# Where the first two block loads are issued, and in which order eight additions stand: a decoder layer on one core

## The chip, the cores and the metric

One core of a Trainium2 chip runs the whole program. The metric is the device time in microseconds. All products run on TensorE (PE); VectorE (DVE), ScalarE (ACT) and GpSimd (POOL) prepare and finish them; SyncE (SP) issues nearly all loads. Each engine works through its own instructions in order, and waits for others by semaphores.

## The reference

One layer of a post-norm decoder on 256 tokens of width 2048, in float32:

```python
def reference(x, w_in, ...):
    ...
    mixed = token_mixers(x, l, w_in[l], ...)   # sparse attention, mLSTM, differential attention
    x = layer_norm(ALPHA * x + jnp.einsum('bse,ed->bsd', mixed, w_out[l]), ln1_g[l], ln1_b[l])
    h = jnp.square(jax.nn.relu(jnp.einsum('bsd,df->bsf', x, w_up[l])))
    x = layer_norm(ALPHA * x + jnp.einsum('bsf,fd->bsd', h, w_down[l]), ln2_g[l], ln2_b[l])
```

The sparse attention scores all keys with a small indexer (8 heads) and keeps the 64 best of each query. The feed-forward part is 8192 wide.

## The kernel before

**Split products.** Each 1 MB piece of a weight is loaded by SP into a buffer `raw` (`load_raw`, L100; three buffers). `split_to` (L107) makes two float32r halves of it: ACT casts `hi` (L108), DVE subtracts `lo = raw - hi` (L109). Both have four buffers. PE multiplies `hi` and `lo` with the split activations. A unit of transposed output (`unit_t`, L203, products L211 and L212) or of normal output (`run_units`, L247, L261 to L263) takes a weight in two halves, and after each half `tick()` moves small work on: whatever a head has put off with `later`, and one step of `block_sums`:

```python
def tick():                     # L87
    ...
    if clock[0] > START:        # L93
        next(blocks, None)
```

**The index.** Early on, while the values of the sparse attention are projected (weights `w_va0`, then `w_va`), the indexer's scores are summed up on DVE (L302, L304). Then, for two blocks of 128 queries, eight rounds of MAX (L314) and MATCH_REPLACE (L315) find the 64 best; POOL masks before and behind them (L310, L317), and the first head's scores need the result (L382).

**Block sums.** The second half of `w_down`'s columns is multiplied in a scheme of seven products for eight (Strassen's form), which needs sums of blocks of the weights. For the first three groups (`AHEAD`) they are made while the mixers run: 12 jobs (`block_sums`, L139) of four 128x512 blocks each, in a borrowed buffer `lent` with room for two jobs. A job loads four blocks (L146), subtracts four times on DVE (L154), one step each, and stores the sums in DRAM (L157); then it loads the job two later. `pin` fixes the order of the pinned instructions among themselves as they are traced; everything else a scheduler may move.

**The feed-forward part.** In each of the groups `g` 0 to 6, `w_up` units of the next group ("U") alternate with products of this one. For g below 3 the second pair of columns (p = 1) takes its sums from DRAM (`ready_steps`, L989); each product of that pair that isn't kept goes by an accumulating DMA on POOL into `acc`, held in `rx`, or into `macc`, held in `ry` (L962). From g = 3 on the second pair is done by plain products (`plain`). The eight additions that end the second pair are `pair_sums(1)` (L997, additions L1007 to L1017). They are traced in group 3, two a step behind its third step; not being pinned, the scheduler put them earlier. `make_blocks` and `make_sums` split the new group's activations (L911, and L109 into `ms`). `up` ends with half sums (L873, L874), relu and square. `pair_steps` forms the first pair's weight sums on DVE (L973 to L984); L958 adds a product to `acc`.

Of the kernel before, what the change touches and what calls it, by code (L numbers as in the profile page):

```python
# [14 lines left out]
ALU = mybir.AluOpType  # L15
# [9 lines left out]
FG = 8  # L25
FT = DFF // P // FG
TOPK = 64
START = 8
AHEAD = 3
ALPHA = 2.0 ** 0.25  # L30
EPS = 1e-5
# [33 lines left out]
def trunk_kernel(ctx: ExitStack, tc: tile.TileContext, xT, x, w_qi, w_t, w_va0, w_va, w_vm0, w_vm, w_vc,  # L65
                 w_oam, w_oc, w_up4, w_up, w_down, w_dnl, conv, bif, gm, gc, lamv, g1, b1, g2, b2, out):
    nc = tc.nc
# [19 lines left out]
    def tick():  # L87
# [3 lines left out]
        for f in due:  # L91
            f()
        if clock[0] > START:  # L93
            next(blocks, None)
# [42 lines left out]
    pin = tc.keep_in_program_order  # L137

    def block_sums():  # L139
        jobs = [(n // 4, slice(512 * (n % 4), 512 * (n % 4) + 512), [lent[:, 4 * (n % 2) + i, :] for i in range(4)])  # L140
                for n in range(4 * AHEAD)]

        def load(n):
            for g, cs, room in jobs[n:n + 1]:
                for r, (c, i) in zip(room, ((2, 0), (3, 0), (3, 1), (2, 1))):
                    pin(nc.gpsimd.dma_start(r, w_down[g, c, i][:, cs]))  # L146

        load(0)
        load(1)
        for _ in range(4):  # L150
            yield
        for n, (g, cs, (b11, b12, b22, b21)) in enumerate(jobs):
            for d, x, y in ((b12, b12, b11), (b22, b22, b12), (b11, b22, b11), (b21, b21, b22)):
                pin(nc.vector.tensor_sub(d, x, y))  # L154
                yield
            for i, b in enumerate((b12, b22, b11, b21)):
                nc.gpsimd.dma_start(sums_d[g][i][:, cs], b)  # L157
            load(n + 2)
            for _ in range(3):
                yield  # L160

    blocks = block_sums()


# [161 lines left out]
    for c in range(2):  # L326

        n = 452 - 64 * c
# [152 lines left out]
    for c in range(4):  # L481
        n = VM_N[c]
# [481 lines left out]
    def out_block(p, t, c):  # L964
        return acc[:, t, 1024 * p + 512 * c:1024 * p + 512 * c + 512]
# [31 lines left out]
    def pair_sums(p):  # L997

        m = macc
        if p == 0:  # L1000
            raw = wp.tile([P, 2048], F32, tag="raw", name="raw", bufs=3)
            m = raw.rearrange("p (i n) -> p i n", i=4)
            for i, j in KEPT.items():
                nc.scalar.copy(m[:, j], kept[i])
        p1, p5, p6, p7 = (m[:, j] for j in range(4))
        (c11, c12), (c21, c22) = ([out_block(p, t, c) for c in range(2)] for t in range(2))
        nc.vector.tensor_add(p6, p6, p1)  # L1007
        nc.vector.tensor_add(p7, p7, p6)
        yield
        nc.vector.tensor_add(p6, p6, p5)  # L1010
        nc.vector.tensor_add(p5, p5, p7)
        yield
        nc.vector.tensor_add(c11, c11, p1)
        nc.vector.tensor_add(c12, c12, p6)
        yield
        nc.vector.tensor_add(c21, c21, p7)
        nc.vector.scalar_tensor_tensor(c22, c22, ALPHA, p5, ALU.mult, ALU.add)  # L1017
        yield

    def plain(g, c):  # L1020
# [34 lines left out]


    second = pair_sums(1)
    FIRST = "UUUababUabUababUabUabU"
    TURNS = "UUUaaaUcaaaUdUaUU"
# [19 lines left out]
    for _ in pair_sums(0):  # L1079
        pass  # L1080
# [89 lines left out]
```

## Time and profile before

| | |
|---|---|
| time, median of 3 runs | 1181.27 us (1180.67 to 1181.89) |
| the profiled execution | 1182.09 us |
| its span, first to last instruction | 1180.4 us |
| PE busy | 1156.2 us, 98% |
| DVE busy | 913.9 us, 77% |
| ACT busy | 667.2 us, 57% |
| POOL busy | 80.4 us, 7% |
| mean granted clock of PE | 0.991 |
| data read and written | 244.91 and 14.69 MB |

Times of instructions count from the start of the span. A row of a timeline gives the start, the duration, the engine, the line, and in brackets the idle time before the instruction and what ended it. A row with several instructions (x4) runs from the first one's start to the last one's end.

### The profile page before, as it was taken

The numbers are of one execution on the slowest core, as the hardware profiler recorded it, in microseconds if no ns is written. First come the engines' busy times: TensorE is split into PE (matmuls) and PEld (weight loads), VectorE is DVE, ScalarE is ACT, GpSimd is POOL, SyncE is SP. The second block draws the span as 40 slices with busy tenths as digits, with TensorE's granted clock in tenths as the row PEclk, the third lists the DMA queues.
The fourth block names the chain that finished last, engine by engine and source line by source line (L and its number), as shares of the span: only waits on it lengthen the run. The fifth ranks groups of instructions, "written<-read, shape, count | busy, mean of one in ns | idle before, by whom it ended". The sixth has DMA issues, their size and how long they took to land.

```text
span 1180.4 us, 15757 instructions
## 1 busy us (share of the span) xinstructions
PE 1156.2 (98%) x5966; PEld 988.4 (84%) x5966; DVE 913.9 (77%) x1261; ACT 667.2 (57%) x955; POOL 80.4 (7%) x142
## 2 busy tenths in 40 slices
PE   9989999999999999999999999989999999999996
PEld 8878899888888888888888888878888888888885
DVE  5587767798776769859889889879679679688767
ACT  5534454754555454466676777655565475475641
POOL 1031223211000001000000001000000000000002
PEclk9989999999999999999999999989999999999998
DMA  8578779896664564655767967945645636643461
GB/s 320 192 255 289 243 255 330 316 319 219 273 244 155 178 228 164 249 190 203 271 228 212 348 211 247 307 155 175 233 163 194 236 140 215 228 163 126 164 245 72
DMA packets 45785, 264.30 MB, mean 224 GB/s; under 512 B 6022, under 2 KB 6412, under 8 KB 20748
## 3 DMA queue, kind: packets, MB, share of 16 engines
q1 hardware_dynamic: 34716, 227.10, 54.2%
q0 software_dynamic: 10272, 33.04, 8.6%
q10 hardware_dynamic: 720, 3.15, 0.7%
q8 instruction: 47, 0.77, 0.3%
q14 instruction: 30, 0.25, 0.1%
HBM read 244.91 MB, written 14.69 MB: 220 GB/s over the span
## 4 chain that ended last, share of the span: by engine, by line
PE 71%; issue 16%; DVE 7%; DMA 3%; ACT 1%; POOL 1%; DVEq 0%; POOLq 0%; ACTq 0%; SPq 0%
PE ps L211 24%; PE ps L212 13%; DVE lo L109 3%; PE pst L263 3%; PE pst L261 3%; PE pst L262 3%; PE pst L1035 3%; PE pst L1034 3%; PE pst L1033 2%; PE psl L722 2%; PE psl L724 2%; PE psl L725 2%; PE pk L942 1%; PE pk L944 1%; PE pk L943 1%
## 5 line engine op out<-in xcount | busy, mean ns | idle before, releaser
L109 DVE TENSOR_TENSOR lo<-raw,hi 128x1024 fp32r<-128x1024 f32 (+5 forms) x370 | 437.4, 1190 | 177.2 <-ACT hi L108 176.1
L108 ACT CAST hi<-raw 128x1024 fp32r<-128x1024 f32 (+5 forms) x371 | 377.8, 1023 | 340.7 <-PE ps L211 151.3
L211 PE MATMUL ps<-xs,hi 128*128 128x512 f32 x1472 | 522.0, 395 | 0.0
L212 PE MATMUL ps<-xs,lo 128*128 128x256 f32 x1472 | 418.2, 284 | 10.5 <-DVE lo L109 10.4
L211 PEld LDWEIGHTS ps<-xs,hi 128*128 128x128 f32 x1472 | 278.5, 189 | 58.6 <-issue 0.3
L212 PEld LDWEIGHTS ps<-xs,lo 128*128 128x128 f32 x1472 | 280.3, 190 | 16.0 <-DVE lo L109 14.6
L109 DVE TENSOR_TENSOR lo<-b,hi 128x1024 fp32r<-128x1024 f32 x84 | 101.1, 1222 | 15.8 <-ACT hi L108 15.7
L108 ACT CAST hi<-b 128x1024 fp32r<-128x1024 f32 x84 | 88.2, 1051 | 38.4 <-PE pst L1035 16.8
L261 PE MATMUL pst<-hi,xs 128*128 128x384 f32 (+4 forms) x224 | 80.3, 358 | 0.0
L262 PE MATMUL pst<-lo,xs 128*128 128x384 f32 (+4 forms) x224 | 78.9, 352 | 0.6 <-DVE lo L109 0.6
L263 PE MATMUL pst<-hi,xs 128*128 128x384 f32 (+4 forms) x224 | 78.6, 351 | 0.0
L943 PE MATMUL pp<-lo,ms 128*128 128x512 f32 x168 | 66.8, 398 | 1.3 <-DVE lo L109 1.3
L944 PE MATMUL pp<-hi,ms 128*128 128x512 f32 x168 | 66.5, 396 | 0.0
L942 PE MATMUL pp<-hi,ms 128*128 128x512 f32 x168 | 66.4, 396 | 0.0
L1034 PE MATMUL pst<-lo,ms 128*128 128x512 f32 x128 | 50.6, 395 | 0.0
L1035 PE MATMUL pst<-hi,ms 128*128 128x512 f32 x128 | 50.6, 395 | 0.0
L1033 PE MATMUL pst<-hi,ms 128*128 128x512 f32 x128 | 50.1, 395 | 0.0
L261 PEld LDWEIGHTS pst<-hi,xs 128*128 128x128 f32 x224 | 42.2, 188 | 3.5 <-issue 0.7
L262 PEld LDWEIGHTS pst<-lo,xs 128*128 128x128 f32 x224 | 42.1, 188 | 3.0 <-DVE lo L109 1.2
L942 PE MATMUL pk<-hi,ms 128*128 128x512 f32 x112 | 44.6, 398 | 0.0
L944 PE MATMUL pk<-hi,ms 128*128 128x512 f32 x112 | 44.5, 397 | 0.0
L943 PE MATMUL pk<-lo,ms 128*128 128x512 f32 x112 | 44.5, 397 | 0.0
(298 smaller groups left out, 1587.3 us busy)
## 6 DMA issues: line engine op xcount, KB each, us to landing
raw<-in_w_up_dram SPq DMA_DIRECT2D x64, 1024.0 KB, 4.9
raw<-in_w_t_dram SPq DMA_DIRECT2D x32, 1024.0 KB, 6.0
raw<-in_w_down_dram SPq DMA_DIRECT2D x25, 1024.0 KB, 4.9
b<-in_w_down_dram SPq DMA_DIRECT2D x21, 1024.0 KB, 5.1
lent<-in_w_down_dram POOLq DMA_DIRECT2D x48, 256.0 KB, 6.8
sums<-lent POOLq DMA_DIRECT2D x48, 256.0 KB, 4.1
raw<-in_w_oam_dram SPq DMA_DIRECT2D x12, 1024.0 KB, 4.8
raw<-sums SPq DMA_DIRECT2D x12, 1024.0 KB, 5.9
```

The source lines that it names most:

```text
L108: nc.scalar.copy(hi, src)
L109: eng.tensor_sub(lo, src, hi.bitcast(F32))
L211: nc.tensor.matmul(ps, hi[:, P * kk:P * kk + P], xs[:, k, :], start=(k == 0), stop=False)
L212: nc.tensor.matmul(ps[:, 0:S], lo[:, P * kk:P * kk + P], xs[:, k, 0:S], start=False, stop=(k == KT - 1))
L261: nc.tensor.matmul(pss[t][:, :n], a_hi, w_hi, start=first, stop=False)
L262: nc.tensor.matmul(pss[t][:, :n], a_hi, w_lo, start=False, stop=False)
L263: nc.tensor.matmul(pss[t][:, :n], a_lo, w_hi, start=False, stop=last)
L942: nc.tensor.matmul(ps, forms[:, f, 0, k, :], w_hi, start=first and k == 0, stop=False)
L943: nc.tensor.matmul(ps, forms[:, f, 0, k, :], w_lo, start=False, stop=False)
L944: nc.tensor.matmul(ps, forms[:, f, 1, k, :], w_hi, start=False, stop=last and k == HT - 1)
L1034: nc.tensor.matmul(pss[t], forms[:, f, 0, k, :], w_lo, start=False, stop=False)
L1035: nc.tensor.matmul(pss[t], forms[:, f, 1, k, :], w_hi, start=False, stop=last)
```

## The change

`block_sums` loads its first two jobs on SP's queue, where the weights are, and no longer on POOL's. START falls from 8 to 4, and each of the two loads is followed by four steps, so that the loads stand eight and four steps ahead of the first subtraction; that one keeps its step in the traced order. All later loads stay on POOL. In `pair_sums`, the additions of the second pair (p = 1) are pinned: they keep their order as traced against the other pinned instructions. Those of the first pair are not.

```diff
@@ -25,7 +25,7 @@
 FG = 8
 FT = DFF // P // FG
 TOPK = 64
-START = 8
+START = 4
 AHEAD = 3
 ALPHA = 2.0 ** 0.25
 EPS = 1e-5
@@ -140,15 +140,15 @@
         jobs = [(n // 4, slice(512 * (n % 4), 512 * (n % 4) + 512), [lent[:, 4 * (n % 2) + i, :] for i in range(4)])
                 for n in range(4 * AHEAD)]
 
-        def load(n):
+        def load(n, eng=nc.gpsimd):
             for g, cs, room in jobs[n:n + 1]:
                 for r, (c, i) in zip(room, ((2, 0), (3, 0), (3, 1), (2, 1))):
-                    pin(nc.gpsimd.dma_start(r, w_down[g, c, i][:, cs]))
-
-        load(0)
-        load(1)
-        for _ in range(4):
-            yield
+                    pin(eng.dma_start(r, w_down[g, c, i][:, cs]))
+
+        for n in range(2):
+            load(n, nc.sync)
+            for _ in range(4):
+                yield
         for n, (g, cs, (b11, b12, b22, b21)) in enumerate(jobs):
             for d, x, y in ((b12, b12, b11), (b22, b22, b12), (b11, b22, b11), (b21, b21, b22)):
                 pin(nc.vector.tensor_sub(d, x, y))
@@ -1004,17 +1004,19 @@
                 nc.scalar.copy(m[:, j], kept[i])
         p1, p5, p6, p7 = (m[:, j] for j in range(4))
         (c11, c12), (c21, c22) = ([out_block(p, t, c) for c in range(2)] for t in range(2))
-        nc.vector.tensor_add(p6, p6, p1)
-        nc.vector.tensor_add(p7, p7, p6)
+
+        keep = pin if p else lambda i: i
+        keep(nc.vector.tensor_add(p6, p6, p1))
+        keep(nc.vector.tensor_add(p7, p7, p6))
         yield
-        nc.vector.tensor_add(p6, p6, p5)
-        nc.vector.tensor_add(p5, p5, p7)
+        keep(nc.vector.tensor_add(p6, p6, p5))
+        keep(nc.vector.tensor_add(p5, p5, p7))
         yield
-        nc.vector.tensor_add(c11, c11, p1)
-        nc.vector.tensor_add(c12, c12, p6)
+        keep(nc.vector.tensor_add(c11, c11, p1))
+        keep(nc.vector.tensor_add(c12, c12, p6))
         yield
-        nc.vector.tensor_add(c21, c21, p7)
-        nc.vector.scalar_tensor_tensor(c22, c22, ALPHA, p5, ALU.mult, ALU.add)
+        keep(nc.vector.tensor_add(c21, c21, p7))
+        keep(nc.vector.scalar_tensor_tensor(c22, c22, ALPHA, p5, ALU.mult, ALU.add))
         yield
 
     def plain(g, c):
```

SP, at the start of the program. `raw` are weight buffers, `lent` the blocks of the first two jobs; the weights of width 1808 are `w_va0`, those of 1552 `w_va`.

```order
-L104 DMA raw<-in_w_va_dram 128x1808 x4
+L104 DMA raw<-in_w_va_dram 128x1808 x3
+L146 DMA lent<-in_w_down_dram 128x512 x4
+L104 DMA raw<-in_w_va_dram 128x1808
+L104 DMA raw<-in_w_va_dram 128x1552
+L146 DMA lent<-in_w_down_dram 128x512 x4
+L104 DMA raw<-in_w_va_dram 128x1552 x3
 L346 DMA convt<-in_conv_dram 128x48
 L348 DMA bift<-in_bif_dram 128x12
```

Two groups of four block loads now stand among the weights of `w_va0` and `w_va`; four small loads (two shown) moved behind the last of `w_va`.

DVE, in the selection of the index. `m` are the eight maxima of a round, `rx` the scores; the first `lo` is the first half of the first `w_t` unit, the last one (+) its second half.

```order
+L109 TENSOR_TENSOR lo<-raw,hi 128x1024
+L314 MAX m_589<-rx 128x8
 L314 MAX m_677<-rx 128x8
-L315 MATCH_REPLACE rx<-m_585,rx 128x128
+L315 MATCH_REPLACE rx<-m_589,rx 128x128
 L315 MATCH_REPLACE rx<-m_677,rx 128x256
 L316 TENSOR_SCALAR rx<-rx 128x128
 L314 MAX m_680<-rx 128x8
-L109 TENSOR_TENSOR lo<-raw,hi 128x776
+L109 TENSOR_TENSOR lo<-raw,hi 128x1024
```

The second half's `lo` of width 1024 now stands behind one and a half rounds of the second block of queries (128x256); before, it stood behind five and a half. The four L154 stand ahead of all these rows now, the first among the scores' sums (L304); before, they stood one by one in the second block's fourth and fifth rounds, ahead of this `lo`.

DVE, in group 3 of the feed-forward part, from the third `lo` on. `b_7130` and `b_7129` are blocks of the first pair's weights, `ry` holds the second pair's kept sums.

```order
+L1009 TENSOR_TENSOR ry<-ry 128x512
+L109 TENSOR_TENSOR lo<-b_7130,hi 128x1024
+L1010 TENSOR_TENSOR ry<-ry 128x512
+L874 TENSOR_TENSOR half<-ps,half 128x256
+L109 TENSOR_TENSOR lo<-b_7130,hi 128x1024
+L1012 TENSOR_TENSOR ry<-ry 128x512
+L109 TENSOR_TENSOR lo<-b_7129,hi 128x1024
+L1013 TENSOR_TENSOR ry<-ry 128x512
+L958 TENSOR_TENSOR rx<-rx,pp 128x512
+L109 TENSOR_TENSOR lo<-b_7129,hi 128x1024
+L109 TENSOR_TENSOR lo<-raw,hi 128x1024
+L976 TENSOR_TENSOR b_7129<-b_7129,ry 128x2048
```

The additions, which stood some 20 to 60 DVE instructions earlier, are now laced between the splits of the first pair's weights. Behind these rows follow L958, L1015, L1016 and the `lo` of the next up unit's second half, and after that unit's L874 the last two, L1018 and L1019.

## Rows read from the trace of the kernel before

**Rows 1.** The page: PE's busy time; the block loads, KB, us to landing.

```profile
PE 1156.2 (98%) x5966; PEld 988.4 (84%) x5966; DVE 913.9 (77%) x1261; ACT 667.2 (57%) x955; POOL 80.4 (7%) x142
...
lent<-in_w_down_dram POOLq DMA_DIRECT2D x48, 256.0 KB, 6.8
```

**Rows 2.** Waits of PE, whole span: us in total, times, longest us.

```profile
PE ps L212 <- DVE lo L109: 10.4, 6, 4.9
```

**Rows 3.** Timeline of PE, first pause: start us, us, instruction, idle before.

```profile
74.36 0.39 PE L211 MATMUL ps<-xs,hi 128*128 128x512 f32 x1
...
74.71 0.39 PE L211 MATMUL ps<-xs,hi 128*128 128x512 f32 x1
79.99 0.58 PE L212 MATMUL ps<-xs,lo 128*128 128x256 f32 x1 [4.89 <-DVE lo L109]
80.37 0.63 PE L211 MATMUL ps<-xs,hi 128*128 128x512 f32 x1
...
81.01 0.63 PE L211 MATMUL ps<-xs,hi 128*128 128x512 f32 x1
...
84.85 0.49 PE L211 MATMUL ps<-xs,hi 128*128 128x512 f32 x1
```

**Rows 4.** Windows: us, busy us by engine, granted clock, DMA share, GB/s.

```profile
80.00:82.00 2.00, 2.00 (x6) 1.79 (x7) 2.00 (x4) 0.00 (x0) 0.52 (x1) 0.50 0.83 236
212.00:216.00 4.00, 3.44 (x19) 2.88 (x18) 2.25 (x4) 3.96 (x7) 2.67 (x5) 1.00 0.83 300
```

**Rows 5.** Timeline of DVE around the first pause.

```profile
55.60 1.71 DVE L304 SCALAR_TENSOR_TENSOR rx<-relu,rx 128x128 f32<-128x128 f32 x4
...
70.27 0.42 DVE L314 MAX8 m<-rx 128x8 f32<-128x256 f32 x1
...
71.25 0.43 DVE L314 MAX8 m<-rx 128x8 f32<-128x256 f32 x1
74.84 0.69 DVE L154 TENSOR_TENSOR lent<-lent 128x512 f32<-128x512 f32 x1 [3.17 <-DMA lent<-in_w_down_dram]
...
78.73 1.21 DVE L109 TENSOR_TENSOR lo<-raw,hi 128x1024 fp32r<-128x1024 f32 x1
```

**Rows 6.** Timeline of POOL: issue of the first two jobs' block loads.

```profile
67.93 4.43 POOL L146 DMA_DIRECT2D lent<-in_w_down_dram  x8
```

**Rows 7.** Timeline of PE, second pause and behind it.

```profile
763.40 0.50 PE L943 MATMUL pp<-lo,ms 128*128 128x512 f32 x1 [0.50 <-DVE lo L109]
...
789.24 0.58 PE L212 MATMUL ps<-xs,lo 128*128 128x256 f32 x1 [4.28 <-DVE lo L109]
...
794.95 0.44 PE L942 MATMUL pk<-hi,ms 128*128 128x512 f32 x1
...
806.60 0.28 PE L212 MATMUL ps<-xs,lo 128*128 128x256 f32 x1
```

**Rows 8.** Timeline of DVE around the second pause.

```profile
773.75 0.69 DVE L1016 TENSOR_TENSOR rx<-rx,ry 128x512 f32<-128x512 f32 x1 [3.73 <-DMA rx<-new]
...
787.03 0.42 DVE L874 TENSOR_TENSOR half<-ps,half 128x256 f32<-128x256 f32 x1
...
799.63 2.29 DVE L976 TENSOR_TENSOR b<-b,ry 128x2048 f32<-128x2048 f32 x1
801.84 0.68 DVE L958 TENSOR_TENSOR rx<-rx,pp 128x512 f32<-128x512 f32 x1
802.44 1.22 DVE L109 TENSOR_TENSOR lo<-raw,hi 128x1024 fp32r<-128x1024 f32 x1
...
804.17 4.62 DVE L109 TENSOR_TENSOR lo<-raw,hi 128x1024 fp32r<-128x1024 f32 x4
```

**Rows 9.** DMA issues in 25 to 27.5 us: fourth load of w_va0.

```profile
raw<-in_w_va_dram SPq DMA_DIRECT2D x1, 904.0 KB, 4.7
```

**Rows 10.** Timeline of ACT: the first cast of that load.

```profile
38.08 0.95 ACT L108 CAST hi<-raw 128x904 fp32r<-128x904 f32 x1 [1.53 <-PE pst L263]
```

**Rows 11.** Timeline of SP: the last two loads of w_va.

```profile
42.67 5.05 SPq L104 DMA_DIRECT2D raw<-in_w_va_dram  x2
```

## Prediction

> **What bounds the kernel now.** I read the page first: PE is busy 1156.2 us, 98% of the 1180.4 us span [rows 1], and its products are the same before and after, so only PE's pauses and its time at the low clock can be won. The waits of PE come next: nearly all of its waiting is for `lo`, the second half of each weight split, which DVE makes: 10.4 us in six waits, the longest 4.9 [rows 2]. The timeline of PE finds the two long ones, 4.89 us before 79.99 [rows 3] and 4.28 us before 789.24 [rows 7]; no other is over 1 us. The reader should see that each pause costs twice. Behind the first, the granted clock is 0.50, the lower of the two levels, 1.2 against 2.4 GHz [rows 4], and a pair of products (L211, L212) goes from 0.35 us (74.36 to 74.71) to 0.64 us (80.37 to 81.01) until 84.85 [rows 3].
>
> Then DVE's timeline says why `lo` was late. At 74.84 the first block subtraction (L154) had waited 3.17 us for its blocks to land, and the `lo` that PE needed stood behind it and came at 78.73 [rows 5]. POOL had issued the blocks only from 67.93 on, all eight in a row [rows 6]. At 773.75 an addition of the second pair's sums (L1016) had waited 3.73 us for an accumulating transfer into the same output block [rows 8]. Both are waits of an in-order engine for a DMA, with PE's work behind them.
>
> **The change part by part, in the profiled execution's time (1182.09 us, span 1180.4; 0.82 us above the median of 1181.27).**
>
> First pause. The first two jobs' blocks go out on SP 20 us and more before they are used, so the 3.17 us wait goes. The four subtractions are also spread ahead of where they stood, as is the `gct` scaling (L614). That is work on a full DVE, so I follow the `lo` that was late. It started at 78.73; take off the wait, 3.17, and the four rounds of MAX and MATCH_REPLACE that, by the order shown with the change, now stand behind it, 0.98 each (70.27 to 71.25) [rows 5]: 71.6. Add at most 0.69 for L614, priced as the subtraction of the same width [rows 5]: 72.3, done 1.21 later at 73.5. PE wants it behind the product that starts at 74.71 [rows 3], so PE, which stood idle from 75.1 (79.99 - 4.89), would find it there 1.6 us early. The subtractions themselves cancel: they stood before this `lo` and still do. I take the whole pause, **4.9 us**, and its low clock: 79.99 to 84.85 is 4.86 us, of which 1 - 0.35/0.64 = 45% comes back, **2.2 us**.
>
> What pays for it: SP issues eight more DMAs, four behind the third load of w_va0 and four behind the first of w_va. The fourth w_va0 load stands behind the first four. Its 904 KB took 4.7 us to land and were issued before 27.5 [rows 9], so they were there by 32.2; ACT casts them at 38.08, when PE frees a buffer [rows 10]. That is 5.9 us of cover. The blocks are 1024 KB, by the same row 5.3 us, if all of it adds: inside the cover, nothing. The second four meet an emptier queue. Without the cover, each microsecond would be one of PE's. The small loads of conv, gates, gm and `gct` now stand behind the last w_va load, issued by 47.7 [rows 11]; `gct` is the fourth, and even 6.8 us to landing, the slowest kind of load in the rows [rows 1], after two more microseconds of issue gives 56.5; DVE scales it among the L304s that run from 55.60 to 57.31 and now start a subtraction later [rows 5]. At worst a fraction of a microsecond, with PE still ahead: nothing. On POOL the job's stores now stand ahead of the index selects, and three loads of the third job ahead of one; what waits for that select comes some 10 us later. Nothing.
>
> Second pause. The eight additions leave the stretch before 776 and stand among group 3's first steps, some 20 us later, where the last accumulation has long landed. The wait of 3.73 goes, and so does the late `lo`: **4.3 us** for the pause, and 789.24 to 794.95 at the low clock, 5.71 x 45% = **2.6 us** [rows 7]. The small wait of 0.50 at 763.40 [rows 7] is fed by the same additions: **0.5 us**.
>
> The additions are not free in the new place. From the `lo` that ends the pause to the one that starts the second half of the next up unit, DVE now has eight `lo` (4.62/4 = 1.15 us each), six of the eight additions and two L958 (801.84 to 802.44, 0.60 each), L976 (799.63 to 801.84, 2.21) and one L874 (0.42) [rows 8]: 9.2 + 4.8 + 2.2 + 0.4 = 16.6 us. PE covers the same stretch from 789.24 to 806.60, 17.4 us, less the 2.6 of low clock: 14.8 us [rows 7]. If DVE enters level with PE, PE must wait **1.8 us** there. The ends: 0 if DVE enters 1.8 us ahead, and a pause as long as the present one, 4.3 us with 2.6 of low clock, if it enters behind. DVE's chain ahead of it is tied to PE's own units (L874 reads what PE has just finished), so level is the nearest. Does such a pause lower the clock? In 212 to 216 PE idled 0.56 us in all and the clock stayed 1.00 [rows 4]; both pauses over 4 us lowered it. 1.8 is nearer the first, and I take no low clock.
>
> Sum: 4.9 + 2.2 + 4.3 + 2.6 + 0.5 - 1.8 = **12.7 us**. From the profiled execution that is 1169.4; from the median, 1181.27 - 12.7 = **1168.6 us**.
>
> **The rivals.**
>
> DVE has slack in the new place. The 1.8 us are not paid: 1181.27 - 14.5 = 1166.8. For it: `lo` has four buffers, so DVE may run ahead by that many. Against: the count above starts level.
>
> The first stretch stays tight. DVE is busy without a gap there, and a selection round or a store that slips makes `lo` late. The 3.17 us of wait are surely gone; if the four rounds do not help, `lo` comes 3.9 us later, at 77.4, and PE waits 77.4 - 75.1 = 2.3 us: 1170.9.
>
> The pause moves with the additions. If DVE enters the new place behind, the pause of 4.3 and its 2.6 return in place of the 1.8: 1168.6 + 5.1 = 1173.7.
>
> No change: both stretches are bound by DVE's work, not by its waits, and both pauses come back whole: 1181.3. Against: 3.17 + 3.73 us of DVE idling stand in the rows.
>
> Slower: SP is in order, and its loads feed every product. If each block load held the queue until it landed, 6.8 us each [rows 1], four would keep the next weights 27.2 us; less 5.9 of cover, PE idles 21.3 us, twice, 42.6 us: 1168.6 + 42.6 = 1211. It decides from the point where a group of four holds the weights longer than 5.9 us. Against: POOL issued eight such loads in 4.43 us [rows 6], far less than one takes to land, so they overlap. The Trainium skill, "DMA: Bandwidth & Descriptors", section "Two DMAs through the same engine are not ordered", says that descriptors of one queue start in order but are pipelined. By that rule the group costs the weights its transfer and not four landings, which speaks against this rival; the overlap on POOL agrees, and no row here shows four such loads on SP.
>
> **How the numbers follow.** 0.62 for the forecast, 0.10 for slack in the new place, 0.12 for a tight first stretch, 0.09 for the moved pause, 0.04 for no change, 0.03 for slower. The first three hold 0.84 between 1166.8 and 1170.9. The range opens them by 0.8 below, the distance between the profiled execution and the median, and by 1.6 above, some half way to the moved pause: 1166.0 to 1172.5. A difference under 0.2% (2.4 us) could not be told from none. Faster by more than that: all but the last two, 0.93; same 0.04; slower 0.03.
>
> **What would show it.** Right: DVE's first L154 stands near 56 us and waits for no DMA; PE has no pause near 75 us and the granted clock stays at 1.00 there; L1009 to L1019 (their new lines) run from about 779 us on without a DMA wait; PE's waits fall from 10.4 us to 2 or 3, the largest near the second half of the up unit behind the additions. Wrong: a wait of DVE or ACT for a load of weights between 28 and 50 us; a wait of L614 for `gct`; a pause of over 3 us, with the clock at 0.50 behind it, in either stretch.

## The result, and the profile after

| | before | after |
|---|---|---|
| median of the runs of the comparison | 1181.58 us (4 runs) | 1168.25 us (1168.21 to 1168.47, 4 runs) |
| ratio, 95% interval | | 0.9883 (0.9866 to 0.9901) |
| the profiled execution, its span | 1182.09, 1180.4 us | 1168.47, 1166.8 us |
| mean granted clock of PE | 0.991 | 0.997 |

The change makes the kernel 1.17% faster, 13.3 us between the medians. The forecast was 1168.6 us.

The page of the changed kernel and its waits of PE (us in total, times, longest us) answer to [rows 1, 2]: PE is busy for 6.3 us less, most of it because nothing in the two stretches now runs at the low clock, and `lo` makes it wait 2.0 us where it was 10.4.

```profile
PE 1149.9 (99%) x5966; PEld 982.6 (84%) x5966; DVE 913.2 (78%) x1261; ACT 668.0 (57%) x955; POOL 78.6 (7%) x134
```

```profile
PE ps L212 <- DVE lo L109: 2.0, 3, 1.6
PE psk L243 <- ACT hi L108: 1.9, 2, 1.5
```

**First stretch.** The timeline of PE (start us, us, instruction) has no pause where [rows 3] had 4.89 us: the product that started at 79.99 starts at 75.72, 0.23 us behind the one ahead of it, and the one that started at 84.85 starts at 78.27. The windows (columns as in [rows 4]) give the clock.

```profile
75.49 0.39 PE L211 MATMUL ps<-xs,hi 128*128 128x512 f32 x1
75.72 0.28 PE L212 MATMUL ps<-xs,lo 128*128 128x256 f32 x1
...
78.27 0.39 PE L211 MATMUL ps<-xs,hi 128*128 128x512 f32 x1
```

```profile
76.00:78.00 2.00, 2.00 (x14) 1.76 (x13) 1.97 (x5) 0.63 (x1) 0.56 (x1) 1.00 0.97 356
```

DVE's timeline answers to [rows 5]: the first block subtraction stands at 56.70 and waits for nothing, `gct` (L614) neither, and the `lo` of the second half starts at 72.34, where 78.73 stood.

```profile
56.70 0.69 DVE L154 TENSOR_TENSOR lent<-lent 128x512 f32<-128x512 f32 x1
57.30 0.35 DVE L304 SCALAR_TENSOR_TENSOR rx<-relu,rx 128x128 f32<-128x128 f32 x1
57.57 0.42 DVE L614 TENSOR_SCALAR gct<-gct 128x512 f32<-128x512 f32 x1
...
72.34 1.21 DVE L109 TENSOR_TENSOR lo<-raw,hi 128x1024 fp32r<-128x1024 f32 x1
```

SP's timeline shows the two groups of block loads among the weights, and `gct` at the end; ACT's shows the cast of the fourth `w_va0` load, the one behind the first group.

```profile
25.20 2.67 SPq L146 DMA_DIRECT2D lent<-in_w_down_dram  x4
27.96 7.07 SPq L104 DMA_DIRECT2D raw<-in_w_va_dram  x2
35.08 1.87 SPq L146 DMA_DIRECT2D lent<-in_w_down_dram  x4
38.56 10.01 SPq L104 DMA_DIRECT2D raw<-in_w_va_dram  x3
...
50.11 0.43 SPq L591 DMA_DIRECT2D gct<-in_gc_dram  x1
```

```profile
38.93 0.95 ACT L108 CAST hi<-raw 128x904 fp32r<-128x904 f32 x1 [1.53 <-PE pst L263]
```

The cast still waits for PE, as in [rows 10], and not for its load.

**Second stretch.** PE's timeline: the products of [rows 7] that started at 763.40, 789.24, 794.95 and 806.60. The 4.28 us are gone; a new pause of 1.61 stands ahead of the last.

```profile
755.39 0.40 PE L943 MATMUL pp<-lo,ms 128*128 128x512 f32 x1
...
776.45 0.37 PE L212 MATMUL ps<-xs,lo 128*128 128x256 f32 x1
...
779.56 0.40 PE L942 MATMUL pk<-hi,ms 128*128 128x512 f32 x1
...
792.86 0.39 PE L212 MATMUL ps<-xs,lo 128*128 128x256 f32 x1 [1.61 <-DVE lo L109]
```

DVE's timeline answers to [rows 8]: from the `lo` at 775.16 to the one at 791.59 (four in a row; PE waits for the first) it has no gap, and no addition waits for a DMA.

```profile
775.16 1.22 DVE L109 TENSOR_TENSOR lo<-raw,hi 128x1024 fp32r<-128x1024 f32 x1
776.29 2.36 DVE L109 TENSOR_TENSOR lo<-b,hi 128x1024 fp32r<-128x1024 f32 x2
778.57 0.69 DVE L1009 TENSOR_TENSOR ry<-ry 128x512 f32<-128x512 f32 x1
...
786.45 1.22 DVE L109 TENSOR_TENSOR lo<-raw,hi 128x1024 fp32r<-128x1024 f32 x1
787.58 2.29 DVE L976 TENSOR_TENSOR b<-b,ry 128x2048 f32<-128x2048 f32 x1
...
790.98 0.69 DVE L1016 TENSOR_TENSOR rx<-rx,ry 128x512 f32<-128x512 f32 x1
791.59 4.63 DVE L109 TENSOR_TENSOR lo<-raw,hi 128x1024 fp32r<-128x1024 f32 x4
```

Two windows give the clock: in the kernel before it was 0.50 behind the second pause (first row); in the changed kernel it stayed at 1.00 around the new one (second row).

```profile
790.00:792.00 2.00, 2.00 (x8) 1.66 (x7) 2.00 (x3) 0.00 (x0) 0.00 (x0) 0.50 0.70 176
```

```profile
791.00:794.00 3.00, 1.39 (x8) 1.03 (x7) 3.00 (x5) 0.75 (x1) 0.00 (x0) 1.00 0.19 27
```

### The profile page after: what moved, and what is told of

Its sections match the earlier page's. It is cut to its first block, busy times and chain, and to the rows that moved or that the text cites. A ratio compares the mean times of both kernels' runs of the same rounds, so it can differ in the third digit from the quotient of the medians.

```text
span 1166.8 us, 15751 instructions
## 1 busy us (share of the span) xinstructions
PE 1149.9 (99%) x5966; PEld 982.6 (84%) x5966; DVE 913.2 (78%) x1261; ACT 668.0 (57%) x955; POOL 78.6 (7%) x134
## 4 chain that ended last, share of the span: by engine, by line
PE 87%; DVE 6%; DMA 3%; issue 2%; ACT 1%; SPq 0%; DVEq 0%; ACTq 0%
PE ps L211 27%; PE ps L212 15%; PE pst L261 4%; PE pst L262 4%; PE pst L263 4%; DVE lo L109 4%; PE pst L1037 3%; PE pst L1036 3%; PE pst L1035 2%; PE pp L943 2%; PE pp L944 2%; PE pp L942 2%; PE psl L722 2%; PE psl L724 2%; PE psl L725 2%; PE pk L942 2%
```

## The experiments

All are compared with the kernel before by the ratio of their times; its median in the four groups of runs was 1181.58, 1182.12, 1180.75 and 1182.31 us.

### The loads alone

```diff
-        keep = pin if p else lambda i: i
+        keep = lambda i: i
```

> Only the loads are changed; the eight additions stay unpinned, as before. Theory (two separate waits of DVE for a DMA, each paid by PE as a pause and a stretch at the low clock): the first pause goes with its low clock, 4.9 + 2.2 = 7.1 us, the second stays with 4.3 + 2.6; time 1181.5 - 7.1 = 1174.4 us, clock once at 0.50 near 785 us. Rival (the two are one: the loads' change alone relieves DVE for the whole run): near 1168.3 us and no second pause. Rival (the additions did it all): near 1181.5 us.

Measured: 1173.89 us (1172.24 to 1176.81, 5 runs), ratio 0.9936 (0.9913 to 0.9959). Its waits, of PE and of DVE: the second pause and the wait of an addition for the accumulating DMA are back, nothing is left of the first.

```profile
PE ps L212 <- DVE lo L109: 5.0, 5, 4.3
```

```profile
DVE rx L1018 <- DMA rx<-new: 3.9, 1, 3.9
```

### The pinned additions alone

The kernel before, with the part of the diff that stands in `pair_sums` and without the rest.

> Only the eight additions are pinned; the block loads stay on POOL, as before. Theory: the first pause stays, 4.89 us with the clock at 0.50 behind it; the second goes and 1.6 us come in the additions' new place: 1181.5 - 4.3 - 2.6 - 0.5 + 1.6 = 1175.7 us. Rival (the loads' change did it all): near 1181.5 us. The gains of this and of the loads-only kernel should add up to the whole change, 13.3 us.

Measured: 1175.23 us (1174.3 to 1178.03, 7 runs), ratio 0.9944 (0.9928 to 0.996). The mirror image: L154 waits for its blocks again and PE has its first pause, 5.3 us here; the second is gone and the new one of 1.6 us is there. The two parts gain 0.64% and 0.56%; the whole change gained 1.17%. They add: the two stretches lie 700 us apart, and with either part alone the other's pause stays nearly what it was (4.3 us for 4.28, 5.3 for 4.89).

```profile
74.80 0.69 DVE L154 TENSOR_TENSOR lent<-lent 128x512 f32<-128x512 f32 x1 [3.60 <-DMA lent<-in_w_down_dram]
```

```profile
PE ps L212 <- DVE lo L109: 7.2, 4, 5.3
```

### The queue, without the earlier step

Both loads on SP, traced together four steps ahead of the first subtraction, as before.

```diff
-START = 4
+START = 8
...
-            for _ in range(4):
-                yield
+        for _ in range(4):
+            yield
```

> The loads are on SP's queue, but not earlier: START is 8 again and both loads are traced four steps ahead of the first sum, as before; the additions are pinned. Theory (what counts is the queue: SP reaches the loads between two weight loads, long before POOL gets past the index selects, wherever the step stands): as the whole change, 1168.3 us within 0.6. Rival (the eight and four steps ahead are what counts): the first subtraction waits again, PE pauses near 75 us, 1173 to 1175.5 us.

Measured: 1167.54 us (1167.43 to 1169.46, 4 runs), ratio 0.988 (0.9857 to 0.9903), 0.2 us below the theory's range and not to be told from the changed kernel; PE's waits for `lo` are the same 2.0 us, with no pause near 75 us. SP issues all eight in a row, from 22 us ahead of the first subtraction (55.75) on:

```profile
34.11 4.30 SPq L146 DMA_DIRECT2D lent<-in_w_down_dram  x8
```

So on SP's queue the earlier step is not needed.

### The earlier step, without the queue

```diff
-            load(n, nc.sync)
+            load(n)
```

> The changed kernel with the first two jobs' block loads at their new steps, but on POOL's queue. The four of the first job then stand ahead of POOL's first select, those of the second job still behind it, and the gct scaling stands early again. Theory (the loads have only to be on their way before the select and its wait; which queue carries them doesn't count): L154 waits for no DMA near 57 us, PE's pause near 75 us is 0 to 1.4 us, and the time is 1168.3 to 1169.7 us. Rival (SP's queue is what makes the blocks come in time): L154 waits some 3 us again, PE's pause near 75 us is over 3 us with the clock at 0.50 behind it, and the time is 1174 us or more.

Measured: 1170.71 us (1169.48 to 1171.89, 4 runs), ratio 0.9916 (0.9901 to 0.9931). The rival is out, since L154 waits for nothing near 58 us and PE has no pause near 75 us. But the time is 1.0 us above the theory's upper end. POOL, which has done its small work by then, issues the first job's loads at once, among the first weights of the program:

```profile
4.20 2.33 POOL L146 DMA_DIRECT2D lent<-in_w_down_dram  x4
```

In its first 25 us the seven `raw` loads of 512 KB take a median of 11.1 us to land, against 8.9 in the changed kernel, with the DMA engines' share at 1.0 from 10 to 20 us in both. Here is one of PE's waits that follow, in the index projection; the same product starts at 17.52 in the changed kernel.

```profile
19.10 0.39 PE L244 MATMUL psk<-xs,lo 128*128 128x256 f32 x1 [0.76 <-DVE lo L109]
```

By 22 us PE stands 1.7 us behind the changed kernel's profile. That is more than profiles differ there otherwise: the other eleven of this document lie within 1.3 us of each other at that product, and the changed kernel's is the latest of them. This execution (1171.89 us, the slowest of its four) loses more between 200 and 225 us, where small pauses come and go from profile to profile.

### The same on POOL's queue, but held back

DVE first writes one element of each block's buffer, so that POOL must wait for it.

```diff
-            load(n, nc.sync)
+            load(n, [pin(nc.vector.memset(r[:, 0:1], 0.0)) for r in jobs[n][2]] and nc.gpsimd)
```

> As the run with the early loads on POOL's queue, but each of the two groups is held back until DVE has written one element of each block's buffer (four small MEMSETs a group, traced at the load's step, so some 35 us into the program for the first). Theory (POOL lost in that run because it sent the blocks at 4.2 us, among the first weights, and not because of its queue): the first block loads are issued near 35 us, the index projection's products near 17 us stand within 1 us of where they stand in the changed kernel, PE has no pause over 1.5 us near 75 us, and the time is 1168.3 to 1169.8 us. Rival (the early loads have no part in it, and POOL's block loads cost time in themselves): 1170.5 us or more, with the excess at another place.

Measured: 1167.99 us (1165.79 to 1168.52, 4 runs), ratio 0.9876 (0.9861 to 0.989), 0.3 us below the theory's range: as fast as the change, with the first job's loads on POOL and no pause of PE near 75 us.

```profile
35.76 2.33 POOL L146 DMA_DIRECT2D lent<-in_w_down_dram  x4 [31.47 <-DVE lent L149]
```

The index projection's products stand 1.3 us earlier than in the changed kernel, no later (18.80 for 20.06; the run with the early loads has 21.75). (Here `gct` makes L614 wait 4.1 us at 46.31; PE has no wait there.) So neither queue nor step matters in itself. SP at the old step is enough. POOL at the new step is enough, if it is held off the first weights. Only POOL at the old step, as in the kernel before, is late. What matters is when the first job's blocks travel: behind the starved first 20 us, and ahead of the selects at 57 us that hold POOL's queue. (The second job's loads, behind a select at 72.88 here, are not waited for.) SP's queue does both without a wait of its own.

### All block loads on SP

```diff
-        def load(n, eng=nc.gpsimd):
+        def load(n, eng=nc.sync):
```

> The changed kernel with the block loads of all twelve jobs on SP's queue. The later jobs' loads wait there until the stores of the sums have left their buffers, and the weights' loads stand behind them. Theory (a group of four costs the weights its transfer alone, and the buffers of the weights cover a short wait): 1167.5 to 1170.5 us, with at most one or two pauses of PE of 1 to 2 us between 90 and 400 us. Rival (block loads hold the queue of the weights until they land, 5 us and more for each of the ten further groups beyond what the buffers cover): waits of ACT and DVE for raw and PE pauses of 5 us and more a group, 1190 us and above.

Measured: 1171.93 us (1170.79 to 1174.08, 4 runs), ratio 0.9932 (0.9916 to 0.9949). Ten more groups on SP cost 3.7 us in all by the medians (0.5% by the ratios), nothing like 5 us a group, so the rival is out; yet the time is 1.4 us above the theory's range. The cost has a place. SP's own waits (first row), DVE's and PE's:

```profile
SPq L146 <- DMA sums<-lent: 61.8, 13, 11.6
```

```profile
199.39 0.56 DVE L477 SCALAR_TENSOR_TENSOR rx<-rx,negm 128x384 f32<-128x384 f32 x1 [5.26 <-DMA rx<-rows]
```

```profile
208.02 0.44 PE L261 MATMUL pst<-hi,xs 128*128 128x384 f32 x1 [2.27 <-ACT hi L108]
```

A later job's load waits for the store that empties its buffer, 11.6 us in one case, and SP stands still meanwhile. A small load of the attention (`rows` into `rx`) behind it is issued at 190.77 instead of 187.20; DVE, then ACT's cast, then PE are late: with two shorter waits beside the one shown, PE loses 4.3 us against the changed kernel from 201 to 209 us. Block loads on SP are free only while their buffers are.

### Four more operations on DVE in the new place

```diff
+        for _ in range(2 * p):
+            keep(nc.vector.tensor_max(p6, p6, p6))
```

in each of the first two steps of `pair_sums`.

> The changed kernel with four more DVE operations of the same width (the maximum of a sum with itself, which leaves its values as they are) among the first two steps of the second pair's final additions. Theory (the new pause of 1.6 us is DVE's work minus PE's in that stretch, with no slack to take up more): each of the four adds 0.60 us, the pause near 793 us grows from 1.6 to 4.0 us, and the time is 1170.7 us if the clock stays at 1.00 behind it, 1173.3 us if it falls to 0.50 as it did behind the pauses of 4.3 and 4.9 us. Rival (DVE has slack there and something else makes the pause): the pause stays 1.6 us and the time 1168.3 us.

Measured: 1174.94 us (1173.02 to 1175.64, 4 runs), ratio 0.9949 (0.9934 to 0.9964). The pause grows, as the theory says, but to 5.0 us, not 4.0, and the time is 1.6 us above the 1173.3 that it gave for a fall of the clock. Timelines of PE and DVE, and the windows:

```profile
794.49 0.58 PE L212 MATMUL ps<-xs,lo 128*128 128x256 f32 x1 [5.00 <-DVE lo L109]
```

```profile
775.34 1.22 DVE L109 TENSOR_TENSOR lo<-raw,hi 128x1024 fp32r<-128x1024 f32 x1
...
793.22 4.62 DVE L109 TENSOR_TENSOR lo<-raw,hi 128x1024 fp32r<-128x1024 f32 x4
```

```profile
795.00:797.00 2.00, 2.00 (x8) 1.71 (x7) 2.00 (x3) 0.00 (x0) 0.00 (x0) 0.50 0.50 70
799.00:801.00 2.00, 2.00 (x13) 1.79 (x12) 1.79 (x2) 1.05 (x1) 0.00 (x0) 1.00 0.99 401
```

DVE's part came as priced: the second half's `lo` is now the second of the four, 1.13 behind 793.22, that is 19.0 us behind 775.34 where the changed kernel has 16.4, and four times 0.60 is 2.4. But the scheduler also moved the first half's `lo` behind the additions (786.45 above), so PE stops a half unit earlier and waits longer; just ahead, at 787.59, it also waits 0.9 us for a cast of ACT. Behind the long pause the clock is 0.50, and the product at 798.97 stands 8.46 us later than its counterpart in the changed kernel (790.51), against 6.41 at 794.49 (788.08): 2.1 us for the low clock. The rival (slack on DVE) is out.

### The additions five steps later

```diff
-            elif n > 2 and g == AHEAD:
+            elif n > 7 and g == AHEAD:
```

> The whole change, with the pinned additions begun five steps later in group 3 (from step 8 on in place of step 3). Theory (the 1.6 us pause is DVE's work in that stretch, 16.6 us against PE's 14.8, and DVE has slack later): the pause goes and none comes, 1168.3 - 1.6 = 1166.7 us. Rival (DVE is full in all of the group): the pause moves along with the additions, 1168.3 us. Rival (the pause has another cause, such as the first pair's block loads): it stays where it is, 1168.3 us.

Measured: 1166.04 us (1165.54 to 1166.49, 4 runs), ratio 0.9863 (0.9841 to 0.9886), the fastest kernel here: these four runs and the four of the next experiment all lie below the eight of the changed kernel, though the intervals of the ratios overlap. The new pause is gone, and the additions stand where DVE has room:

```profile
787.49 0.38 PE L212 MATMUL ps<-xs,lo 128*128 128x256 f32 x1 [0.17 <-DVE lo L109]
...
790.37 0.28 PE L212 MATMUL ps<-xs,lo 128*128 128x256 f32 x1
```

```profile
801.01 0.69 DVE L1009 TENSOR_TENSOR ry<-ry 128x512 f32<-128x512 f32 x1
```

The second row is the counterpart of 792.86 above and waits for nothing; the first, half a unit ahead of it, has the only wait of the stretch.

### Both late

The edits of "the queue, without the earlier step" and "the additions five steps later" together.

> The changed kernel with both edits that held alone: both block loads traced together four steps ahead of the first subtraction, still on SP, and the second pair's final additions five steps later. Theory (the two act in separate stretches, so their effects add): the first run of the later additions gave 1166.04 us and the first edit alone was within 0.7 us of the changed kernel, so 1165.3 to 1166.1 us, with no PE pause over 1 us in either stretch. Rival (one undoes the other, by a place that the scheduler moves): 1167.5 us or more.

Measured: 1166.17 us (1165.58 to 1166.79, 4 runs), ratio 0.9877 (0.9863 to 0.9892); 0.07 us above the theory's range, and not to be told from the additions alone. The loads' step is worth nothing that can be measured.

### The changed kernel once more

> The changed kernel once more, nothing edited. What differs between its two profiles is variation from run to run: if the small differences between the kernels' profiles that no changed instruction explains (0.85 us before 20 us, pauses of 0.56 and 0.75 us between 212 and 228 us) are such variation, then they differ between these two profiles by as much, and the time is 1167.6 to 1168.9 us. If they belong to the change, both profiles show them alike, within 0.2 us.

Measured: 1168.93 us (1166.81 to 1170.22, 4 runs), ratio 0.9891 (0.9874 to 0.9907), just above the expected range. The differences before 20 us are variation: a product at 20.06 in the other profile stands at 18.97 in this one, 1.1 us ahead. A 0.76 us pause at 227.10 in the kernel before is missing in both profiles of the changed kernel, which by the text would make it the change's. It is missing as well in the kernel with the pinned additions alone, whose edit is in group 3, some 500 us behind it, and it is there at 223.12 in the kernel with the early loads on POOL and at 218.97 in the one with the later additions. So it comes and goes, and this experiment's rule was too simple for it.

## Why the prediction was right

Each term can be read from the start of the same product in the two traces, counted from the first.

| term | predicted | measured | from the starts |
|---|---|---|---|
| first pause | 4.9 | 5.05 | 74.71 to 75.49 is +0.78; 79.99 to 75.72 is -4.27 |
| its low clock | 2.2 | 2.31 | 84.85 to 78.27 is -6.58 |
| small wait | 0.5 | 0.66 | 762.50 to 755.15 is -7.35; 763.40 to 755.39 is -8.01 |
| second pause | 4.3 | 4.56 | 784.45 to 776.22 is -8.23; 789.24 to 776.45 is -12.79 |
| its low clock | 2.6 | 2.60 | 794.95 to 779.56 is -15.39 |
| new pause | -1.8 | -1.65 | 806.60 to 792.86 is -13.74 |
| sum | 12.7 | 13.53 | the last product is 13.6 earlier |

What lies between the terms (0.8 us lost before 20 us, 1.6 won between 85 and 230, 0.9 lost by 615, 0.2 won between 763 and 784) nearly cancels, and at least the first changes from profile to profile of one kernel.

- **Both waits were DMA waits of DVE, and both went.** The first L154 and the additions wait for nothing; each part of the change alone brings back the other's pause. (A later job's L154 still waits, 3.2 us at 193.34 and 2.3 at 199.11 before, with no pause of PE above 0.6 us in the 20 us behind it: such a wait counts only where `lo` has no slack.) No run takes a wait away and leaves DVE's order as it was, so how much of each pause was the wait, and how much the work that moved with it, is not shown.
- **How the second wait reached PE.** The prediction took this pause whole and did not follow its `lo`. The half sum L874 at 777.24 stood behind L1016 and L1017; ACT waited for it (first row, the kernel before; second row, the changed kernel), ACT's next cast stood behind that, and DVE in turn waited 1.42 us for the cast. From there DVE needs the same 8.9 us to the `lo` in both kernels (779.08 to 787.97, 766.27 to 775.16). In the changed kernel that `lo` was done only 0.07 us before PE took it up: that the whole pause went was in part luck. Two earlier additions had waited as well, 2.15 us at 743.47 and 1.34 at 760.79; the latter stood ahead of the `lo` of the small wait.

```profile
777.69 0.42 ACT L875 ACTIVATE half<-half 128x256 f32<-128x256 f32 x1 [5.98 <-DVE half L874]
```

```profile
764.87 0.42 ACT L875 ACTIVATE half<-half 128x256 f32<-128x256 f32 x1 [1.35 <-DVE half L874]
```

- **The first `lo`.** Predicted to start at 72.3 and be done at 73.5; it started at 72.34. Taking off the wait and the four rounds that passed behind it, and adding L614, was enough.
- **What was costed at nothing.** The weights: SP spent 2.67 and 1.87 us on the two groups, and between 28 and 50 us no cast waited for its load. `gct`, issued at 50.11, was there when DVE took it up at 57.57. The third job's three loads ahead of a select cost PE nothing: it has no pause there.
- **The new pause.** DVE's 16.6 us were 16.4 (775.16 to 791.59), PE's 14.8 were 14.8 (776.45 to 792.86 - 1.61 = 791.25), and DVE entered level: its `lo` was done by 776.38, 0.07 us ahead of PE. The rival "slack in the new place" failed on that, and the four added operations showed that more work there goes into PE's pause. That the clock would hold was chosen and not derived; it held.
- **The pauses were worth a little more than their rows.** They were worth 0.2 and 0.3 us more. A wait counts from the end of the product ahead, but products overlap: one that lasts 0.39 is followed by the next after 0.23 when nothing is late (75.49 to 75.72), so 0.16 us more is lost at the first pause. Ahead of the second the product lasts 0.50 (first row, the kernel before), and in the changed kernel the next one follows after 0.23 (776.22 to 776.45, second row): 0.27 more.

```profile
784.45 0.50 PE L942 MATMUL pk<-hi,ms 128*128 128x512 f32 x1
```

```profile
776.22 0.40 PE L942 MATMUL pk<-hi,ms 128*128 128x512 f32 x1
```

- **The slower rival.** Eight loads on SP took 4.30 us to issue, where one takes 6.3 us to land (median in the changed kernel), so they were not awaited one by one; the next weight was issued 0.1 us behind the first four (27.96). The rule of the Trainium skill, "DMA: Bandwidth & Descriptors", section "Two DMAs through the same engine are not ordered", that within one queue of a DMA engine descriptors start in order and are pipelined, agrees with these rows. The rival has a true core that the prediction did not see: a load whose buffer is not yet free does hold SP, 11.6 us at worst, as the run with all loads there showed.

The prediction named SP's queue and the 20 us of lead together as the cure. The runs separate them: the lead comes from standing ahead of POOL's selects; eight steps or four on SP, or POOL at the earlier step, give the same time as long as the first job's blocks leave after the first weights and well before 56 us.

## What to carry to other kernels

When an in-order engine waits for a DMA, look first at what the issuing queue stood behind, and issue from a queue that is free in time, but not before the transfers that are needed first are through. Work that is moved out of a wait is paid for where it lands: count both engines' work from one hand-over to the next, and if the sums are not level, move it on to a stretch where they are (here five steps, 1.6 us). A long pause of PE costs its length and then a stretch at the low clock: here, pauses of 4.3 and 4.9 us were worth half as much again as their rows say.

## What was not expected

- Loads that are not urgent cost 1.7 us of PE when they were issued at 4.20 us, just before the first weights kept the DMA engines full; issued at 35.76, on the same queue, they cost nothing.
- A load that waits for its buffer on SP reached PE by way of a small load of another stage: 3.6 us late at issue, 2.27 us of PE pause some 17 us later.
- Behind the pauses of 1.61 us and, in the run with all loads on SP, 2.27 us the granted clock stayed at 1.00; behind those of 4.28, 4.89 and 5.00 it was 0.50. Where between them it turns was not tried.
